# A hybrid encoder trunk on one core: seven block products in place of eight in seven GEMM stretches, and layer 1 in another order

## The chip, the core and the metric

One core of one Trainium2 chip. PE multiplies into PSUM (8 banks), ACT, DVE and POOL work on the elements, SP, ACT and POOL issue DMAs. The metric is the device time of one execution in microseconds; the kernel before took 1682.24 us (median of 3 runs, 1680.69 to 1684.24).

## The reference, cut to what matters

512 tokens, width 2048, two layers in float32. Layer 0 is latent attention with a gate, layer 1 an mLSTM with gates, each followed by an output projection and `x <- LN(ALPHA * x + y)`.

```
# layer 0: 16 heads; attn [512, 2048], z [512, 2048]
y = (attn * silu(z)) @ w_out                      # 2048 x 2048
x = layernorm(ALPHA * x + y) * ln_w + ln_b
# layer 1: 8 heads of 128 (q, k) and 256 (v)
qk, v, o, gates, z = split(x @ w_in)              # columns: 2048, 2048, 2048, 16, 2048
q, k = split(silu(causal_conv(qk)))
cell = rmsnorm(mlstm_chunkwise(q, k, v, gates))   # per head, decay exponents from the gates
y = (sigmoid(o) * cell * silu(z)) @ w_out
x = layernorm(ALPHA * x + y) * ln_w + ln_b
```

## The kernel before, in words

Every GEMM keeps float32 accuracy with three products: each operand is split into `hi` (rounded to the float32r mantissa) and `lo` (the rest), and `mm3` (L199) issues hi x hi, hi x lo, lo x hi, each a matmul of 128x128 by up to 128x512. `split` (L166) is a cast on ACT (L168) and a subtraction on DVE (L169). The activations stand transposed in SBUF, 16 k tiles of [128, 512 tokens] as `hi`/`lo` pairs (32 tiles of tag `h`). Weights come by SP's queue in units of 512 KB into three `raw` buffers (`weights`, L172) and are split into three `whi`/`wlo` pairs.

There are two loops over units. `gemm_a` (L221) has tokens as rows of the result and 512 columns; a unit of two k tiles serves every token block asked for, 24 matmuls for four blocks, 12 for two. `gemm_b` (L205) has 256 columns as rows of the result and all 512 tokens beside them. Four PSUM banks (`acc`) hold GEMM results, four (`ps`) the rest.

Work of other engines and small matmuls is written as tasks (generators) that `tick` (L116) steps between the parts of a GEMM: a task yields how many us of matmul time its next step should lie ahead. `finish` (L125) runs a task out at once. The framework then puts the instructions of each engine into an order by its own model of the times, so program order is a priority, not the order on the engine; on the chip each engine runs its list in order.

`out_proj` (L585) does four column blocks of 512: blocks 0 and 1 for all tokens, 2 and 3 for tokens 0-255 and then for 256-511, so that the first pair can be normalised (`finish0` L857, `finish1` L928) while the second is multiplied. Its input tiles are made on demand, two ahead (`g0` L881, `g1` L902).

`mlstm` (L798) goes by pairs of heads: values (`v_block`, 512 columns), o and z of the first head (`gate_out`, L694), q, k with the convolution (`conv_silu`, L682), then o and z of the second head. The cells of the two heads (`cell`, L725) are tasks beside the next GEMMs, one at a time. A cell makes four score blocks, four value steps (`values`, L745) and turns the normalised rows (`turn`, L766), multiplying by the gate. Finished heads 0 to 5 go to DRAM and come back in `g1`. The residual of layer 1 is reread from DRAM, scaled and shifted on POOL in `resid1` (L918).

Of the kernel before, what the change touches and what calls it, by code (L numbers as in the profile page):

```python
# [16 lines left out]
P = 128  # L17
# [29 lines left out]
def _pieces(value, bits):  # L47
    """The value as a sum of len(bits) + 1 float32 numbers, the first of so many bits each."""
    out = []
    for b in bits:  # L50
        e = math.floor(math.log2(value)) - b + 1
        p = math.floor(value / 2.0 ** e) * 2.0 ** e
        out.append(p)
        value -= p
    return out + [value]


class Task:
    """Work that is traced between the steps of a GEMM: a generator that yields how many us of TensorE
    time its next step should lie ahead, so that the other engines' work hides behind the GEMM."""  # L60
# [5 lines left out]
class Ahead:  # L66
    """A list whose items are made, in order, some items before they are first asked for."""
# [13 lines left out]
class Kern:  # L81
    def __init__(self, ctx, tc):
# [11 lines left out]
        self.queue, self.active = [], []  # L94

# [5 lines left out]
    def start(self, gen):  # L101
        """A task that takes its first step at once and no place among the others."""
# [57 lines left out]
    def behind(self, ins, after):  # L160
        """Instructions are issued behind earlier ones of their engines."""
# [4 lines left out]
    def split(self, src, hi, lo):  # L166
        """src = hi + lo exactly, hi being src rounded to the float32r mantissa."""
# [4 lines left out]
    def weights(self, src):  # L172
        """src: DRAM [128, kts, ..] of at most 1024 values a partition."""
# [25 lines left out]
    def mm3(self, out, a, b, start, stop):  # L199
        """out += a.T @ b, a and b pairs (hi, lo)."""  # L200
# [4 lines left out]
    def gemm_b(self, w, row0, col0, x, ncol=2, kts=4):  # L205
        """[128 * ncol columns, 512 tokens] as ncol PSUM tiles; x: list of (hi, lo) [128, 512]."""
# [44 lines left out]
    def rsqrt_small(self, a, w=1):  # L251
        """a ** -0.5 of a [128, w] tile."""
# [5 lines left out]
    def newton(self, y, a, t, eng):  # L258
        """One step for y = a ** -0.5; t is scratch."""
# [6 lines left out]
    # ---------------------------------------------------------------- constants  # L266
# [46 lines left out]
    def rope_tables(self, positions):  # L313
        """cos [128, 512] and sign * sin, row p of frequency p % 32."""
# [30 lines left out]
    def rope(self, src, n, use):  # L345
        """Rotates src (PSUM or SBUF, [n, 512], heads of 64 rows) and hands a float32 tile to use."""
# [55 lines left out]
    def mla(self, x, positions, w_in, w_qb, w_kvb, load_params):  # L402
# [34 lines left out]
        # k_rope: hi and lo of the weights side by side as the stationary operand  # L437
# [27 lines left out]
        # the gate path  # L465
# [10 lines left out]
        # attention, four heads at a time  # L476
        qv = w_qb.rearrange("(k p) (h c) -> p k h c", p=P, c=QK)
        kv = w_kvb.rearrange("(k p) (h c) -> p k h c", p=P, c=2 * NOPE)
        for grp in range(H0 // 4):
            hs = slice(4 * grp, 4 * grp + 4)  # L480

            # V in [tokens, 4 heads * 128]
# [17 lines left out]
            for pair in range(2):  # L500
# [34 lines left out]
                for j in range(2):  # L535
# [3 lines left out]
                    g[i] = g[i], self.add(self.attend(qt[j], kt[j], qr[j], (krh, krl), vs, g[i], rot))  # L539
        return g  # L540

    def attend(self, q, k, qr, kr, vs, g, rot):
        """g *= softmax(q k) v, transposed."""
# [37 lines left out]
        nc.vector.tensor_tensor(g, o, g, op=ALU.mult)  # L581

    # ---------------------------------------------------------------- output projection and LayerNorm

    def out_proj(self, w_out, g, resid, finish, last=1):  # L585
# [4 lines left out]
        nc = self.nc  # L590
        r, tasks = {}, []
# [206 lines left out]
    def mlstm(self, w_in, x, gscr, late):  # L798
        """The cells as tasks; late is x for who reads the second pair of token blocks first."""
        tasks = []  # L800
        for pair in range(H1 // 2):
# [11 lines left out]
            if pair == 0:  # L813
                self.finish(rows)
# [158 lines left out]
```

## Time and profile before

| | |
|---|---|
| runs | 1680.69, 1682.24, 1684.24 us |
| profiled execution, first to last instruction (span) | 1679.8 us |
| median of the runs less that span | 2.4 us |
| PE busy / DVE / ACT / POOL | 98 / 54 / 37 / 12% |
| granted TensorE clock, mean | 0.997 |
| DMA moved | 202.77 MB, mean 121 GB/s |

Busy is the time in which an engine had an instruction running; matmuls overlap, so the rate of PE is read from the spacing of their starts. The profiled execution is known by its span. An instruction's line can be that of a helper (L168, L169, L196), so the tile names tell which use it is.

### The profile page before, as it was taken

How to read it: one execution, taken by the hardware profiler on the slowest of the kernel's cores; microseconds unless marked ns; L12 is line 12 of the kernel's file. 1: busy time of each engine (PE TensorE's matmuls, PEld its weight loads, DVE VectorE, ACT ScalarE, POOL GpSimd, SP SyncE). 2: the span in 40 equal slices, each digit the busy share in tenths (PEclk: the TensorE clock that was granted, in tenths of full speed). 3: DMA queues.
4: the chain of work that ended last, by engine and by line, in shares of the span. 5: the costliest groups of instructions: out<-in, count | busy, mean ns of one | idle time of the engine just before them, and what ended most of it. 6: DMA issues, size and time to landing. Idle time of an engine off the chain costs nothing. (4 is left out here: it accounts for less than half of the span.)

```text
span 1679.8 us, 20372 instructions
## 1 busy us (share of the span) xinstructions
PE 1652.9 (98%) x7706; PEld 1374.3 (82%) x7706; DVE 913.6 (54%) x1750; ACT 621.1 (37%) x952; POOL 205.1 (12%) x262
## 2 busy tenths in 40 slices
PE   8999999999999999999999999999999999999996
PEld 7888888888888888788888888888888888888874
DVE  3374222677778535876564524643365524674476
ACT  3343222454556313454334322432243322542232
POOL 1000000000000000110222101220021101336200
PEclk9999999999999999999999999999999999999998
DMA  7333333322223435674435543434535543366364
GB/s 210 105 97 101 92 97 94 101 63 57 72 74 95 138 100 181 199 233 125 123 104 107 102 97 93 109 105 108 99 110 107 98 101 92 125 201 225 130 203 156
DMA packets 173538, 202.77 MB, mean 121 GB/s; under 512 B 21928, under 2 KB 120328, under 8 KB 173440
## 3 DMA queue, kind: packets, MB, share of 16 engines
q1 hardware_dynamic: 161840, 176.84, 39.1%
q0 software_dynamic: 4688, 12.05, 2.5%
q10 hardware_dynamic: 6912, 12.59, 2.4%
q8 instruction: 60, 0.98, 0.2%
q14 instruction: 38, 0.31, 0.1%
HBM read 187.63 MB, written 11.58 MB: 119 GB/s over the span
## 5 line engine op out<-in xcount | busy, mean ns | idle before, releaser
L196 PE MATMUL acc<-h,whi 128*128 128x512 f32 x2496 | 772.9, 391 | 0.0
L169 DVE TENSOR_TENSOR wlo<-raw,whi 128x1024 fp32r<-128x1024 f32 (+1 forms) x311 | 378.6, 1218 | 508.3 <-ACT whi L168 498.0
L168 ACT CAST whi<-raw 128x1024 fp32r<-128x1024 f32 (+1 forms) x311 | 322.8, 1039 | 644.9 <-PE acc L196 563.5
L196 PEld LDWEIGHTS acc<-h,whi 128*128 128x128 f32 x2496 | 465.4, 188 | 94.7 <-issue 1.0
L196 PE MATMUL acc<-whi,h 128*128 128x512 f32 x1520 | 488.6, 393 | 0.0
L196 PE MATMUL acc<-h,wlo 128*128 128x512 f32 x1248 | 486.4, 390 | 0.0
L196 PEld LDWEIGHTS acc<-whi,h 128*128 128x128 f32 x1520 | 285.3, 188 | 58.1 <-ACT whi L168 0.9
L196 PE MATMUL acc<-wlo,h 128*128 128x512 f32 x760 | 297.2, 391 | 4.8 <-DVE wlo L169 4.8
L196 PEld LDWEIGHTS acc<-h,wlo 128*128 128x128 f32 x1248 | 234.5, 188 | 49.7
L196 PEld LDWEIGHTS acc<-wlo,h 128*128 128x128 f32 x760 | 142.9, 188 | 34.2 <-DVE wlo L169 6.9
L255 POOL TENSOR_TENSOR s<-s,mhalf 128x1 f32<-128x1 f32 x40 | 25.9, 647 | 404.9 <-DVE s L607 153.0
L351 POOL DMA_DIRECT2D e<-e x34 | 17.0, 506 | 411.1 <-DVE e L349 310.7
L196 PE MATMUL ps<-h,h 128*128 128x128 f32 (+3 forms) x288 | 60.7, 319 | 0.0
L562 ACT ACTIVATE t<-ps,s 128x128 f32<-128x128 f32 (+3 forms) x64 | 33.7, 527 | 65.2 <-DVE s L561 65.1
L193 PE MATMUL ps<-ident,t 128*128 128x128 f32 x288 | 47.5, 281 | 6.2 <-DMA t<-in_x_dram 6.0
L196 PEld LDWEIGHTS ps<-h,h 128*128 128x128 f32 x288 | 48.5, 189 | 6.3
L709 POOL TENSOR_TENSOR h<-h,e 128x512 f32<-128x512 f32 x16 | 20.6, 1290 | 261.0 <-DVE e L708 261.0
L193 PEld LDWEIGHTS ps<-ident,t 128*128 128x128 f32 x288 | 37.4, 145 | 17.7 <-issue 3.7
L689 POOL TENSOR_TENSOR e<-e,e 128x512 f32<-128x512 f32 x16 | 29.0, 1815 | 164.6 <-ACT e L688 164.6
L196 PE MATMUL acc<-whi,v 128*128 128x512 f32 x128 | 44.0, 402 | 0.0
L196 PE MATMUL acc<-v,whi 128*128 128x512 f32 x128 | 41.8, 406 | 0.0
L168 ACT CAST h<-e 128x256 fp32r<-128x256 f32 (+1 forms) x48 | 22.8, 478 | 47.3 <-POOL e L689 29.5
(184 smaller groups left out, 1342.2 us busy)
## 6 DMA issues: line engine op xcount, KB each, us to landing
raw<-in_ml_w_in_dram SPq DMA_DIRECT2D x136, 512.0 KB, 5.0
raw<-in_mla_w_out_dram SPq DMA_DIRECT2D x48, 512.0 KB, 4.0
raw<-in_ml_w_out_dram SPq DMA_DIRECT2D x48, 512.0 KB, 4.0
raw<-in_mla_w_in_dram SPq DMA_DIRECT2D x47, 512.0 KB, 3.8
t<-in_x_dram SPq DMA_DIRECT2D x16, 256.0 KB, 6.5
raw<-in_mla_w_kvb_dram SPq DMA_DIRECT2D x16, 256.0 KB, 3.2
raw<-in_mla_w_kvb_dram SPq DMA_DIRECT2D x32, 128.0 KB, 2.4
raw<-in_mla_w_qb_dram SPq DMA_DIRECT2D x32, 128.0 KB, 2.3
```

Of the source, the lines that this page charges most:

```text
L168: a = self.nc.scalar.copy(hi, src)
L169: b = self.nc.vector.tensor_tensor(lo, src, hi.bitcast(F32), op=ALU.subtract)
L193: self.nc.tensor.transpose(out, in_, ident)
L196: self.nc.tensor.matmul(out, lhsT, rhs, start=start, stop=stop)
L255: nc.gpsimd.tensor_tensor(y, a, self.mhalf[:, :w], op=ALU.pow)
L351: nc.gpsimd.dma_start(s[r ^ 32 : (r ^ 32) + 32], b[r : r + 32])
L562: nc.scalar.activation(pt[bi], s[:, :n], AF.Exp, bias=b, scale=scale, accum_out=tot)
L689: nc.gpsimd.tensor_tensor(a, a, y, op=ALU.mult)
L709: nc.gpsimd.tensor_tensor(y, y, t, op=ALU.mult)
```

## The change

`quad` multiplies 512 tokens by two column blocks c0 and c1 of 512. The tokens (two halves), the k tiles (even and odd) and the columns (c0, c1) make 2 x 2 blocks, and Winograd's form of Strassen's scheme takes seven block products, p1 to p7, of sums of blocks. `combos` makes the sums of the activations on POOL, once per layer and GEMM input (`S`); the sums of the weights are made on POOL and DVE as the units arrive. The call has three parts of eight units: p1, p3; then p5, p7, p6; then p2, p4. Weight blocks are read again in each part that needs them. The two groups of four PSUM banks change roles from call to call (`banks`).

Seven calls use it: column blocks 1 and 2 of both output projections, values 512 to 1535, and for each of four pairs of heads o (512 columns) with z (512 columns). The rest of the projections stays in `gemm_a` (block 0 whole, block 3 for each half of the tokens).

Layer 1 goes in another order: all values, then all gates, both spilled to DRAM (`vscr` as hi and lo, `ascr` as sigmoid(o) * silu(z) in rows of tokens), then q, k and cells for the four pairs. A cell loads its gate rows and multiplies by them ahead of the turn. The scaled residual is made by a task beside q and k and spilled (`x1r`). Docstrings are removed.

```diff
+    def combos(self, te, to, alloc):
+        G = self.nc.gpsimd
+        a11, a21, a12, a22 = te[:, 0:256], te[:, 256:512], to[:, 0:256], to[:, 256:512]
+        G.tensor_tensor(a11, a21, a11, op=ALU.subtract)
+        G.tensor_tensor(a21, a21, a22, op=ALU.add)
+        G.tensor_tensor(a22, a22, a11, op=ALU.add)
+        G.tensor_tensor(a12, a12, a22, op=ALU.subtract)
+        ...    # te and to are split into hi, lo from alloc()
+    def quad(self, w, c0, c1, x, S, third, done):
+        first, second = self.banks
+        self.banks = second, first
+        def mul(ps, a, i, hl, j):
+            for b in range(2):
+                s = slice(b * P, (b + 1) * P)
+                self.mm3(ps[b], (a[0][:, s], a[1][:, s]), (half(hl[0])[j], half(hl[1])[j]), i == 0, i == KT // 2 - 1)
+            self.tick()
+        p1, p3 = two(first), two(first)
+        for i in range(n):
+            t = raw(blk(2 * i, c0), blk(2 * i + 1, c1))
+            hl = pair()
+            self.split(t, *hl)
+            mul(p1, toks(x[2 * i], 0), i, hl, 0)
+            mul(p3, toks(S[i][1], 0), i, hl, 1)
+        e1 = two(self.t)
+        ...    # e1 <- p1 by ACT
+        e3 = [third(b, p3[b]) for b in range(2)]
+        p5, p7 = two(second), two(second)
+        for i in range(n):
+            t = raw(blk(2 * i, c0), blk(2 * i + 1, c1))
+            b12 = self.e()
+            nc.sync.dma_start(b12, blk(2 * i, c1))
+            b11, b22 = half(t)
+            t2.append(self.t())
+            G.tensor_tensor(b22, b12, b22, op=ALU.subtract)
+            G.tensor_tensor(t2[i], b11, b22, op=ALU.subtract)
+            V.tensor_tensor(b11, b12, b11, op=ALU.subtract)
+            hl = pair()
+            self.split(t, *hl)
+            mul(p5, toks(S[i][0], 1), i, hl, 0)
+            mul(p7, toks(S[i][0], 0), i, hl, 1)
+            if i % 2:
+                ...    # t2[i-1], t2[i] are split side by side; p6 = two(first)
+                    mul(p6, toks(S[i - 1 + j][1], 1), i - 1 + j, hl, j)
+        u2, u5 = two(self.t), two(self.t)
+        for b in range(2):
+            V.tensor_tensor(u2[b], p6[b], e1[b], op=ALU.add)
+        for b in range(2):
+            V.tensor_tensor(u5[b], p5[b], u2[b], op=ALU.add)
+            G.tensor_tensor(e3[b], e3[b], u5[b], op=ALU.add)
+            V.tensor_tensor(u2[b], p7[b], u2[b], op=ALU.add)
+        for b in range(2):
+            done(b, 1, e3[b], None)
+            done(2 + b, 1, u5[b], p7[b])
+        p2, p4 = two(first), two(first)
+        for i in range(n):
+            t = raw(blk(2 * i + 1, c0))
+            b21, t4 = half(t)
+            G.tensor_tensor(t4, b21, t2[i], op=ALU.subtract)
+            ...    # split; p2 and p4 with x[2i+1], tokens 0 and 1
+        for b in range(2):
+            done(b, 0, e1[b], p2[b])
+            done(2 + b, 0, u2[b], p4[b])
     def out_proj(self, w_out, g, S, resid, finish, last=1):
+        plain((0, 1, 2, 3), 0)             # then r[tb, 0] to DRAM
+        def done(tb, col, t, ps):
+            if ps is not None:
+                e = self.e()
+                resid(tb, 1 + col, e)
+                V.scalar_tensor_tensor(e, e, ALPHA, ps, op0=ALU.mult, op1=ALU.add)
+                G.tensor_tensor(t, t, e, op=ALU.add)
+            V.bn_stats(stats[tb][:, 1 + col], t)
+        self.quad(w_out, 512, 1024, g, S, third, done)
+        for toks in ((0, 1), (2, 3)):
+            ...    # r[tb, 0] back from DRAM
+            plain(toks, 3, last if toks[0] else 1)
+            ...    # moments, task finish(toks)
     def mlstm(self, w_in, x, gscr, late, background):
+        self.values_out(w_in, x, 0, (0, 1), vscr)
+        self.values_out(w_in, late, 0, (2, 3), vscr)
+        late.close()
+        combos = self.add(self.mlstm_combos(x, S))   # a step: hi + lo of two tiles on POOL, combos
+        rows = self.start(self.gates(w_in, x))
+        self.values_out(w_in, x, 1536, (0, 1, 2, 3), vscr)
+        self.finish(combos)
+        self.quad(w_in, O_V + 512, O_V + 1024, x, S, copied, value)
+        self.finish(rows)
+        for pair in range(H1 // 2):
+            def gate(tb, col, t, ps):
+                if ps is not None:
+                    nc.vector.tensor_tensor(t, t, ps, op=ALU.add)
+                e = self.e()
+                nc.scalar.activation(e, t, AF.Sigmoid)
+                if col:
+                    nc.gpsimd.tensor_tensor(t, t, e, op=ALU.mult)
+                    z[tb] = t
+                else:
+                    nc.gpsimd.tensor_tensor(t, e, z[tb], op=ALU.mult)
+                    nc.sync.dma_start(at(ascr, tb, pair * 512), t)
+            self.quad(w_in, O_O + pair * 512, O_Z + pair * 512, x, S, copied, gate)
+        self.start(background)             # the residual: 16 tiles, 8 us apart
+        for pair in range(H1 // 2):
+            vs = self.v_block(vscr, pair)  # loads
             q_ps = self.gemm_b(w_in, 0, pair * 256, x)
             ...    # q, k, convolution as before
+                cell = self.cell(hd, q[j], k[j], vs, ascr, out, gscr if pair < 3 else None)
     def cell(...):
+        d = self.decays(hd)
+        ...    # gate rows from ascr on SP
+        yield 5.0
-            V.tensor_scalar(t, hp[:, 0:DV], y, None, ALU.mult)
+            V.scalar_tensor_tensor(t, hp[:, 0:DV], y, gate(tb), op0=ALU.mult, op1=ALU.mult)
-                V.scalar_tensor_tensor(gate[j][:, ts], tp[:, j * P : (j + 1) * P], ...)
+                nc.scalar.activation(out[j][:, ts], tp[:, j * P : (j + 1) * P], AF.Copy, scale=self.head_norm(2 * hd + j))
```

## Rows read from the trace of the kernel before

**Rows 1.** The page, busy time of each engine: us, share of the span, instructions.

```profile
PE 1652.9 (98%) x7706; PEld 1374.3 (82%) x7706; DVE 913.6 (54%) x1750; ACT 621.1 (37%) x952; POOL 205.1 (12%) x262
```

**Rows 2.** Timeline of PE inside a GEMM: start us, us, engine, line, operation, count.

```profile
966.03 0.61 PE L196 MATMUL acc<-h,whi 128*128 128x512 f32 x2
...
966.71 0.61 PE L196 MATMUL acc<-h,whi 128*128 128x512 f32 x2
```

**Rows 3.** Chain of waits, last projection, in order of time: start us, us, what.

```profile
1520.76 95.23 PE acc L196 x420
...
1658.52 1.42 PE acc L196 x5
```

**Rows 4.** Stretches: span, length; busy PE, PEld, DVE, ACT, POOL; clock, DMA share, GB/s.

```profile
586.00:629.00 43.00, 43.00 (x192) 35.59 (x191) 14.24 (x16) 8.27 (x8) 0.00 (x0) 1.00 0.32 101
651.00:673.00 22.00, 22.00 (x99) 18.22 (x98) 12.33 (x14) 8.58 (x9) 0.00 (x0) 1.00 0.61 193
677.00:700.00 23.00, 23.00 (x112) 18.54 (x111) 19.43 (x41) 9.12 (x15) 6.20 (x9) 1.00 0.77 252
1620.00:1680.00 60.00, 43.86 (x187) 34.30 (x185) 46.33 (x82) 13.85 (x15) 3.99 (x4) 0.92 0.51 174
```

**Rows 5.** Timeline of ACT in a half block; in brackets the idle time before.

```profile
653.82 1.05 ACT L168 CAST whi<-raw 128x1024 fp32r<-128x1024 f32 x1 [1.66 <-PE acc L196]
```

**Rows 6.** Timelines of POOL and of DVE where both have two-operand work.

```profile
1468.30 3.44 POOL L924 TENSOR_TENSOR t<-t,h 128x512 f32<-128x512 f32 x2
...
1469.81 0.79 DVE L169 TENSOR_TENSOR h<-g_raw,h 128x512 fp32r<-128x512 f32 x1 [0.39 <-ACT h L168]
...
1528.30 3.54 POOL L924 TENSOR_TENSOR t<-t,h 128x512 f32<-128x512 f32 x2
...
1537.79 3.52 POOL L923 TENSOR_TENSOR t<-t,h 128x512 f32<-128x512 f32 x2
1541.28 2.54 POOL L924 TENSOR_TENSOR t<-t,h 128x512 f32<-128x512 f32 x2
...
1529.95 1.27 DVE L601 SCALAR_TENSOR_TENSOR t<-t,acc 128x512 f32<-128x512 f32 x2
...
1538.55 1.62 DVE L169 TENSOR_TENSOR wlo<-raw,whi 128x1024 fp32r<-128x1024 f32 x1 [3.77 <-ACT whi L168]
```

**Rows 7.** The page, DMA issues: queue, count, KB each, median us to landing.

```profile
raw<-in_ml_w_in_dram SPq DMA_DIRECT2D x136, 512.0 KB, 5.0
...
raw<-in_ml_w_out_dram SPq DMA_DIRECT2D x48, 512.0 KB, 4.0
```

**Rows 8.** Groups by line and form: shapes, count, busy us, mean ns, idle before.

```profile
L169 DVE TENSOR_TENSOR wlo<-raw,whi 128x1024 fp32r<-128x1024 f32 x301 | 371.7, 1236 | 508.3 <-ACT whi L168 498.0 <-DMA raw<-in_mla_w_qb_dram 4.2 <-PE ps L196 4.2
...
L169 DVE TENSOR_TENSOR h<-acc,h 128x512 fp32r<-128x512 f32 x48 | 32.5, 685 | 10.6 <-ACT h L168 10.0
...
L601 DVE SCALAR_TENSOR_TENSOR t<-t,acc 128x512 f32<-128x512 f32 x32 | 21.0, 681 | 10.2 <-PE acc L196 10.1
...
L169 DVE TENSOR_TENSOR h<-e,h 128x256 fp32r<-128x256 f32 x32 | 13.2, 419 | 1.4 <-ACT h L168 1.4
...
L685 DVE TENSOR_SCALAR e<-acc,par 128x512 f32<-128x512 f32 x16 | 12.9, 806 | 5.1 <-PE acc L196 5.1
...
L876 DVE TENSOR_SCALAR e<-ps,par 128x256 f32<-128x256 f32 x24 | 12.7, 538 | 0.0
...
L935 DVE SCALAR_TENSOR_TENSOR t<-t,s,h 128x512 f32<-128x512 f32 x16 | 11.8, 742 | 0.0
...
L861 DVE TENSOR_SCALAR t<-t,s,s 128x512 f32<-128x512 f32 x16 | 8.2, 568 | 0.0
```

**Rows 9.** Timeline of DVE, one value step of the last head.

```profile
1505.62 0.15 DVE L755 COPY s<-ps 128x1 f32<-128x1 f32 x1
...
1509.19 0.48 DVE L764 TENSOR_SCALAR e<-ps,s 128x256 f32<-128x256 f32 x1
```

More of the change, by code (lines that the diff above doesn't have):

```diff
@@ L264, in newton @@
         return y
+    def combos(self, te, to, alloc):
[5 more added lines that the diff above has]
+        G.tensor_tensor(a12, a12, a22, op=ALU.subtract)
+        out = []
+        for t in (te, to):
+            hi, lo = alloc(), alloc()
+            self.split(t, hi, lo)
+            out.append((hi, lo))
+        return out
@@ L580, in attend, with out_proj, plain @@
             self.mm3(o[:, kb * P :], vs[kb], (hi[kb], lo[kb]), kb == 0, kb == NTB - 1)
[L581 to L585 removed]
+        z = g[0]
+        if not there:
+            g[0] = self.e()
+        nc.vector.tensor_tensor(g[0], o, z, op=ALU.mult)
+    def out_proj(self, w_out, g, S, resid, finish, last=1):
         nc = self.nc
+        V, G = nc.vector, nc.gpsimd
         r, tasks = {}, []
         stats = {tb: self.const.tile([P, 4, 6], F32, tag="bn", bufs=4, name=self.name("bn")) for tb in range(NTB)}
[L593 to L594 removed]
+        scr = self.dram.tile([SEQ, 512], F32, name=self.name("rscr"))
+        rows = lambda tb: scr[tb * P : (tb + 1) * P, :]
+        def plain(toks, cb, last=1):
             for tb in toks:
@@ L723, in decays, with cell @@
         return d
-    def cell(self, hd, d, q, k, vs, gate, gscr):
+    def cell(self, hd, q, k, vs, ascr, out, gscr):
         nc, V = self.nc, self.nc.vector
+        d = self.decays(hd)
+        a2 = [self.t().rearrange("p (b c) -> p b c", c=DV) for _ in range(2)]
+        for i in range(2):
+            src = ascr[2 * i * P : (2 * i + 2) * P, hd * DV : (hd + 1) * DV]
+            nc.sync.dma_start(a2[i], src.rearrange("(b p) c -> p b c", p=P))
+        gate = lambda tb: a2[tb // 2][:, tb % 2]
+        yield 5.0
         part = self.part
@@ L800, in mlstm @@
         tasks = []
+        self.start(background)
         for pair in range(H1 // 2):
-            if pair == 0:
-                vs = self.v_block(w_in, x, 0, (0, 1))
-                vs.update(self.v_block(w_in, late, 0, (2, 3)))
-                rows = self.add(self.gates(w_in, x))
-            else:
-                vs = self.v_block(w_in, x, pair, (0, 1, 2, 3))
-            gate = self.gate_out(w_in, x, 2 * pair)
+            vs = self.v_block(vscr, pair)
             q_ps = self.gemm_b(w_in, 0, pair * 256, x)
@@ L812, in mlstm @@
             k = [self.conv_silu(k_ps[j], 8 + 2 * pair + j) for j in range(2)]
-            if pair == 0:
-                self.finish(rows)
             for j in range(2):
                 hd = 2 * pair + j
-                if j:
-                    gate = self.gate_out(w_in, x, hd)
-                cell = self.cell(hd, self.decays(hd), q[j], k[j], vs, gate, gscr if pair < 3 else None)
+                out = [self.h() if hd < H1 - 1 else self.e() for _ in range(2)]
+                cell = self.cell(hd, q[j], k[j], vs, ascr, out, gscr if pair < 3 else None)
                 t = self.add(cell, 0.0 if j else 4.0)
-                tasks.append((t, gate))
+                tasks.append((t, out))
         return tasks
@@ L882, in f, with salloc @@
         def f():
-            t, task = g[i]
-            K.finish(task)
+            K.finish(g[i][1])
+            t = g[i][0]
             hi, lo = K.h(F32R), K.h(F32R)
             K.split(t, hi, lo)
+            if i % 2:
+                S0.append(K.combos(g[i - 1][0], t, salloc(i // 2)))
             return hi, lo
         return f
-    first, second = K.out_proj(mla_w_out[0], Ahead([g0(i) for i in range(H0)], 2), resid0, finish0)
+    def salloc(i):
+        return (lambda: K.v(F32R)[:, :SEQ]) if i in (0, 1, 7) else (lambda: K.h(F32R))
+    S0 = []
+    first, second = K.out_proj(mla_w_out[0], Ahead([g0(i) for i in range(H0)], 2), S0, resid0, finish0)
     K.finish(first)
     K.width = 1
-    cells = K.mlstm(ml_w_in[0], x1, gscr, Turned())
     def bcast(src, cb):
```

188 lines of the change are left out of this document (129 added, 59 removed).

## The prediction

> **What bounds the kernel now.** I read the busy shares first: PE is busy for 98% of the span, POOL for 12% [rows 1]. A busy PE need not be PE at its rate, so next the timeline of PE inside one GEMM: the triple of one `mm3` (its two matmuls on `whi` merged in one row; the one on `wlo` stands between the two rows shown) comes back every 0.68 us, 966.03 to 966.71 [rows 2], so a 128x512 matmul costs 0.227 us. Then the stretches between: through 95.23 us of the last projection, whole and half column blocks alike, the chain of waits is one row of 420 matmuls and nothing else [rows 3], 0.227 us each again, here with the weights as the moving side; it ends at the last matmuls at 1658.5, some 21 us ahead of the end of the span. So the program is PE from end to end, apart from a tail, and a matmul less is 0.227 us less, as long as the other engines keep feeding it. The reader is to see in the windows what feeding means [rows 4]: in a whole block of four token blocks (586 to 629) one weight unit of 512 KB serves 24 matmuls, DVE is busy 14 of 43 us and DMA moves 101 GB/s; in a half block (651 to 673) the same unit serves 12, DVE 12 of 22 us, DMA 193 GB/s, and PE still shows no gap. In that half block ACT waits 1.66 us of each 2.72 (12 matmuls) for PE to give back a weight buffer [rows 5]: the supply is ahead and throttled by PE.
>
> **What it removes.** One `quad` takes two column blocks of 512. Before, that was 8 block products of 48 matmuls (8 k pairs x 2 token blocks x 3), after it is 7. Each call saves 48 x 0.227 = 16 triples x 0.68 = 10.9 us, and there are 7 calls (two projections, one for values, four for gates): **-76.2 us**. The remaining matmuls have the same shape, only the side on which weights stand changes for the gates, and both forms run at 0.227 us [rows 2, 3]. 76.2 us of PE time, 336 matmuls, stay in each call.
>
> **What it adds: the supply of the calls.** First part of a call (p1, p3): 8 units of 512 KB, a split each, 12 matmuls = 2.72 us each. That is the half block of [rows 4] and [rows 5] again; I cost it at nothing, and what hides it is that same PE time.
> Second part (p5, p7, p6): 8 units of 18 matmuls = 4.08 us. Each needs two subtractions on POOL and one on DVE (128x512), the split of 1024 columns, and half of a split of two 512s. No row shows such a mixture, but its pieces are there: POOL's 128x512 two-input operations follow each other at 2.54/2 = 1.25 us when left alone; with a 1024-wide DVE split beside them two of them take 3.52 us, 0.98 more; with two 512-wide splits 3.44 (of which one row is shown, stretched to 0.79), so 0.45 for each; the DVE operations that read PSUM add nothing (3.54 us, although two L601 ran there too, is again one 1024 split) [rows 6]. And DVE's own split stretches from 1.22 to 1.62 beside POOL. So DVE with two SBUF operands and POOL take turns. Their turns add up, per unit: 2 x 1.25 + 0.98 + 2 x 0.45 = 4.38 us against PE's 4.08, so 0.30 x 8 = 2.4 us too much per call.
> Third part (p2, p4): 8 units of 2.72 us, one POOL subtraction and one split: 8 x (1.25 + 0.98) = 17.8 us of turns against 21.8. But the recombination stands there as well: two POOL additions and, in the gate calls, four POOL products (7.5 us); in the projections 2 + 2 additions (5.0 us); for the values two additions and four 512-wide DVE differences (2.5 + 1.8). Sums 25.3, 22.8 and 22.1, over by 3.5, 1.0 and 0.3 us.
> Over the call: gates 5.9, projections 3.4, values 2.7; times 4, 2 and 1 that is 33 us. From it goes the lead with which the second part starts. With three raw and three split buffers the first unit of it can be split some 1.6 us early (its load starts when unit 5 of the first part is split, about 2.3 us into PE's unit 3; landing 4.5, POOL 2.5, DVE 0.7, ACT 1.05 make 11.0 + waits of about 1 = 12.0, PE asks at 13.6): 7 x 1.6 = 11. I take **+22 us**. Below: 0, if recombination products slip behind the operands of later units and the lead is two units. Above: the ring of three raw buffers. A buffer is held for landing (4.0 us for w_out, 5.0 for ml_w_in [rows 7]), 0.4 of issue, POOL 2.6, DVE 0.7, ACT 1.05, DVE 1.22, 10.9 to 12.4 us with short waits, a third of which is 4.1, under the 4.38 above; with a full foreign turn at every step 14, a third 4.67, and in the third part 9.5, a third 3.17 against 2.72: (0.29 + 0.45) x 8 x 7 = 41 more, so 74 at the top.
> The Trainium skill has a rule on this port: "SBUF — State Buffer", section "Who interferes with whom", says that a DVE instruction with two SBUF inputs contends with a GpSimd instruction that reads SBUF, and that the pair is held for the whole instruction. By whole durations a unit of the second part would cost 5.16 us instead of 4.38. The rows agree with the taking of turns and differ in the size, 0.98 added by an operation of 1.24.
>
> **PSUM banks.** p2 finds banks free, p4 takes those of p6. After p6's last matmul DVE needs two additions (0.68 each, as L601 [rows 8]) while PE has p2's six matmuls, 1.36 us: 0.2 us late, 1.4 if a split is just under way. 0.7 x 7 = **+5** (1 to 10). At the other joints the four banks in use were emptied a part earlier.
>
> **Between the layers.** The two half blocks at the end of the projection become one per token pair, so the second pair's normalising comes 22 us after the first's instead of 44. From the first moments to the end of the late values block PE has 3 half blocks = 65 us and 4 us of transposes. DVE has 24 splits of 1.24 = 29.7, the turning of x: 16 x (0.54 + 0.42) = 15.4 and, with half on ACT, 8 x 0.54 + 16 x 0.42 = 11, 16 normalisations of 0.57 = 9.1, and 8 evacuations of 0.7 = 5.6: 71 us [rows 8]. Level with PE; before it was 19.4 of 23 at the worst [rows 4]. **+4** (0 to 8). The sums S for layer 1 (POOL, 8 x (2 x 1.25 + 4 of half the width) = some 42 us plus turns) lie beside 43.5 us of values and 19 us of p1/p3; nothing, at most 8 if that cover is short.
>
> **The cells.** Four pairs of q and k (43.5 us of GEMM) now follow each other with no gate GEMM between. DVE per pair: 8 splits 9.9, four convolutions of four passes of at most 0.81 and a split of 0.69, 3.9 [rows 8], so 15.6, and two cells, each four value steps of 2.2 [rows 9] and some 4 us for scores and their splits (eight operations of 0.3 to 0.7), 12.8: 51 us in 43.5 + 13 of PE. It just fits, **+5** (0 to 15) for cells that arrive late. The residual's POOL work (16 x 2.5 us) moves here from the last projection; POOL, busy for 12% before [rows 1], has room, and behind it stand the cells' decay loads and square roots, each due 5 us ahead or four to a cell. The values and gates come back through SP's queue, 8 and 2 loads of 256 KB a pair and head; what waits on SP behind them are weights with three buffers.
> The last head: the cell starts about 27 us into the last projection's first block instead of at its start, because head 6 is no longer covered by head 7's gates. The block asks for it after six units, 33 us and the cells' own 5. By then the scores are traced; the four value steps (4.07 us from L755 to the end of L764, DVE occupied 2.2 of them [rows 9]: 4.1 + 3 x 2.2), the turn and the split, 13 us, lie beside one unit of 5.4. **+7** (2 to 12).
>
> **The tail.** LayerNorm of the first token pair (8 x 2 x 0.74 = 11.9 us of DVE [rows 8]) had 43.5 us of PE beside it and now has 21.8, where 8 splits take 9.9: 21.8 of 21.8, and the last block waits on splits. **+4** (0 to 10). The 21 us after the last matmul stay.
>
> **Sum**, against the profiled execution's span: 1679.8 - 76.2 + 22 + 5 + 4 + 5 + 7 + 4 = 1650.6. The three runs' median, 1682.24, is 2.4 above that span, so 1653.
>
> **Rivals.**
> (a) The lead hides the supply: parts two and three cost nothing, the other terms at their lower half (12 us): 1682.2 - 76 + 12 = 1618. For it: half blocks of the same DMA rate ran without a gap [rows 3, 4]. Against it: POOL does nothing in those.
> (b) Slower: POOL and DVE block each other for whole instructions. Place: parts two and three of each call. 2.54 for POOL's two, 1.24 and 2 x 0.69 for DVE's [rows 6, 8] make 5.16 a unit, 41.3 us, and 8 x (1.27 + 1.24) + 7.5 = 27.6 for gates (25.1 projections, 25.4 values) against 54.4 of PE: 14.5, 12.0 and 12.3 over, 94 in all; with the other 25 us 1682 - 76 + 119 = 1725. It decides from (76.2 - 25)/7 = 7.3 us a call on; the ring of three raw buffers with full foreign turns, 74 instead of 22, ends on the same side at 1705. For it: 4.38 already exceeds 4.08. Against: 0.98 and 0.45 as measured. (The Trainium skill's page named above states it so.)
> (c) The dense ends (cells, transition, tail) at their upper bounds, 8 + 15 + 12 + 10 = 45 instead of 20: 1678, the gain all but eaten.
> (d) The calls don't save PE time, since small gaps let the granted clock fall from 2.4 to 1.2 GHz as it partly does in the last 60 us (0.92 there [rows 4]): every us at the low level costs half a us. A few gaps of 7 us would have to recur in each call; 1690.
>
> **How the numbers follow.** Forecast 0.50 (its own range 1634 to 1671), (a) 0.22, (b) 0.12, (c) 0.12, (d) 0.04. About 0.2% (3.4 us) is what a measurement of this kernel tells from no change. Faster: all of the forecast and (a), and most of (c): 0.82; same: a sixth of (c) and the edges of (b), 0.04; slower 0.14. The range 1619 to 1690 leaves out the lower part of (a) and the most of (b).
>
> **What would show it.** Right: about 336 matmuls fewer; PE gaps of 0.5 to 5 us at the start of each third part and within the second, behind DVE `wlo` and POOL; POOL two-input operations of 1.3 to 2.3 us filling the second parts; a gap of some 7 us before the last units of the last projection's first block. Wrong: PE unbroken through the calls (a), a second part of over 41 us (b), PE waiting for cells pair after pair (c), a granted clock under 0.97 in the calls (d). The prediction fails if the calls lose under 1 or over 7 us each.

## The result: 1.166 times the time of before

| | us |
|---|---|
| before, median of 4 runs | 1681.82 (1680.69 to 1684.24) |
| after, median of 4 runs | 1960.68 (1957.36 to 1968.47) |
| ratio | 1.1658, interval 1.1633 to 1.1684 |
| predicted | 1653 (1619 to 1690) |

The profiled execution spans 1966.8 us at a mean granted clock of 0.931. The page after, busy shares, slices of the span and chain:

```profile
PE 1688.8 (86%) x7370; PEld 1361.3 (69%) x7370; DVE 1194.8 (61%) x1942; ACT 747.2 (38%) x1187; POOL 625.5 (32%) x600
...
PE   8999999999998898966988788886897788758885
...
PEclk9999999999998998987999989997898899878898
...
PE 42%; DVE 17%; DMA 15%; POOL 13%; issue 7%; ACT 4%; SPq 1%; POOLq 0%; DVEq 0%; ACTq 0%
```

The 336 matmuls are gone (7706 before [rows 1], 7370 now), but from the 13th slice on PE is no longer busy from end to end, and only 42% of the ending chain is PE. From the start times of the matmuls the span can be taken apart: full-rate time (0.227 us for 512 columns), what pauses add, and what intervals near double length add (the spacing of the lower clock level). Before: about 1613 + 14 + 35 us; after: about 1540 + 301 + 105. So some 287 us more went into pauses and 70 into matmuls at the lower clock level.

Windows of the changed kernel (span, length; busy PE, PEld, DVE, ACT, POOL; clock, DMA share, GB/s): second part of the first projection's quad, first part of the values' quad with a long wait in it, second part of the second gate quad, then q, k and cells up to the last q, k matmul, and the first block of the last projection behind it:

```profile
623.00:675.00 52.00, 42.78 (x154) 32.55 (x153) 31.40 (x28) 15.81 (x20) 24.09 (x17) 0.84 0.41 127
...
870.00:923.00 53.00, 25.30 (x86) 18.47 (x85) 26.87 (x24) 17.80 (x27) 35.65 (x33) 0.71 0.47 129
1119.00:1178.00 59.00, 40.37 (x155) 31.41 (x154) 30.94 (x27) 17.20 (x23) 27.59 (x19) 0.83 0.61 111
1420.00:1662.00 242.00, 210.20 (x966) 174.22 (x965) 146.45 (x314) 99.24 (x172) 97.27 (x113) 0.94 0.61 155
1662.00:1800.00 138.00, 89.95 (x400) 71.04 (x399) 90.31 (x264) 61.37 (x139) 49.93 (x76) 0.83 0.38 116
```

The whole column block of [rows 4] had PE busy for 43 of 43 us at clock 1.00. Here no engine is full and the DMAs are not either: a chain of waits, not a rate, in every one. The seven second parts, each from the end of the first part's last matmul to the end of its own last and so with the wait ahead of it, take 50.0, 43.0, 45.1, 56.8, 46.0, 56.6 and 48.3 us, 345.7 together, where I had 8 x 4.08 = 32.6 each and 2.4 more. (The expectations below had a few matmuls of the neighbouring parts in the count, 52 us a part.)

In that of the third gate quad (1227 to 1274) the longest waits are these (us in all, times, longest):

```profile
DVE raw L340 <- POOL t L339: 14.2, 4, 8.5
ACT whi L169 <- DVE raw L340: 13.6, 5, 5.4
POOL raw L338 <- DMA raw<-in_ml_w_in_dram: 11.5, 2, 6.9
```

They make a ring: POOL waits for the load, DVE for POOL, the cast for DVE, and the next load for a buffer that the cast and the split give back. SP's timeline there:

```profile
1221.49 2.06 SPq L304 DMA_DIRECT2D raw<-in_ml_w_in_dram  x4
1233.02 2.61 SPq L335 DMA_DIRECT2D e<-in_ml_w_in_dram  x3
1236.48 1.93 SPq L304 DMA_DIRECT2D raw<-in_ml_w_in_dram  x4
```

And POOL's:

```profile
1227.46 2.54 POOL L338 TENSOR_TENSOR raw<-e,raw 128x512 f32<-128x512 f32 x2 [2.31 <-issue]
1229.96 4.16 POOL L339 TENSOR_TENSOR t<-raw 128x512 f32<-128x512 f32 x3
1241.01 1.30 POOL L338 TENSOR_TENSOR raw<-e,raw 128x512 f32<-128x512 f32 x1 [6.89 <-DMA raw<-in_ml_w_in_dram]
```

SP issues nothing from 1223.6 to 1233.0. In its list the `e` loads of the next three units stand ahead of the first of their `raw` loads, and `e` has three slots, given back by DVE's subtraction. So the units go in batches of three, with a dead time for loading after each.

What a pause does to PE, ahead of the second part of the fourth gate quad, PE's timeline:

```profile
1327.62 0.39 PE L197 MATMUL ps<-whi,h 128*128 128x512 f32 x1
...
1341.27 1.22 PE L197 MATMUL acc<-whi,v 128*128 128x512 f32 x2 [13.25 <-ACT whi L169]
...
1344.19 0.63 PE L197 MATMUL acc<-whi,v 128*128 128x512 f32 x1
...
1344.62 0.63 PE L197 MATMUL acc<-wlo,v 128*128 128x512 f32 x1
...
1345.05 0.55 PE L197 MATMUL acc<-whi,v 128*128 128x512 f32 x1
...
1345.67 0.39 PE L197 MATMUL acc<-whi,v 128*128 128x512 f32 x1
```

After 13 us without work the matmuls come every 0.43 us (1.2 GHz), and every 0.23 us (2.4 GHz) from about 1345.4 on.

### The profile page after: what moved, and what is told of

It is laid out like the page before. It is cut to its first block, busy times and chain, and to the rows that moved or that the text cites. A ratio compares the mean times of both kernels' runs of the same rounds, so it can differ in the third digit from the quotient of the medians.

```text
span 1966.8 us, 21494 instructions
## 1 busy us (share of the span) xinstructions
PE 1688.8 (86%) x7370; PEld 1361.3 (69%) x7370; DVE 1194.8 (61%) x1942; ACT 747.2 (38%) x1187; POOL 625.5 (32%) x600
## 4 chain that ended last, share of the span: by engine, by line
PE 42%; DVE 17%; DMA 15%; POOL 13%; issue 7%; ACT 4%; SPq 1%; POOLq 0%; DVEq 0%; ACTq 0%
PE acc L197 33%; DMA raw<-in_ml_w_in_dram 8%; PE ps L197 8%; DVE wlo L170 7%; ACT whi L169 3%; DMA raw<-in_ml_w_out_dram 2%; PE ps L194 2%; DMA h<-n 1%; DMA raw<-in_mla_w_out_dram 1%; DVE raw L340 1%; POOL raw L367 1%; DVE h L170 1%; POOL e L951 1%; POOL t L339 1%; POOL s L256 1%
## 5 line engine op out<-in xcount | busy, mean ns | idle before, releaser
L170 DVE TENSOR_TENSOR wlo<-raw,whi 128x1024 fp32r<-128x1024 f32 (+1 forms) x351 | 476.0, 1362 | 373.9 <-ACT whi L169 360.6
L197 PE MATMUL acc<-h,whi 128*128 128x512 f32 x1472 | 461.9, 395 | 0.0
L197 PEld LDWEIGHTS acc<-h,whi 128*128 128x128 f32 x1472 | 276.6, 190 | 56.0 <-issue 1.0
L197 PE MATMUL acc<-h,wlo 128*128 128x512 f32 x736 | 288.9, 393 | 0.0
L197 PE MATMUL ps<-whi,h 128*128 128x512 f32 x568 | 192.7, 410 | 20.7 <-ACT whi L169 12.5
L197 PEld LDWEIGHTS acc<-h,wlo 128*128 128x128 f32 x736 | 139.4, 189 | 29.6
L197 PEld LDWEIGHTS ps<-whi,h 128*128 128x128 f32 x568 | 112.7, 199 | 48.3 <-ACT whi L169 16.3
L197 PE MATMUL ps<-wlo,h 128*128 128x512 f32 x284 | 119.2, 420 | 26.9 <-DVE wlo L170 26.9
L367 POOL TENSOR_TENSOR raw<-raw,t 128x512 f32<-128x512 f32 x56 | 82.6, 1486 | 74.8 <-DMA raw<-in_ml_w_in_dram 41.7
L197 PE MATMUL ps<-whi,v 128*128 128x512 f32 x168 | 65.5, 451 | 42.3 <-DVE ones L822 22.7
L197 PEld LDWEIGHTS acc<-whi,v 128*128 128x128 f32 x296 | 59.4, 203 | 47.1 <-ACT whi L169 32.9
L339 POOL TENSOR_TENSOR t<-raw 128x512 f32<-128x512 f32 x56 | 84.6, 1520 | 2.8
```

The source lines that it names most:

```text
L170: b = self.nc.vector.tensor_tensor(lo, src, hi.bitcast(F32), op=ALU.subtract)
L197: self.nc.tensor.matmul(out, lhsT, rhs, start=start, stop=stop)
L339: G.tensor_tensor(t2[i], b11, b22, op=ALU.subtract)
L367: G.tensor_tensor(t4, b21, t2[i], op=ALU.subtract)
```

## The experiments

GpSimd is POOL, VectorE is DVE, the array is PE. The theories: A, the latency of the weight sums' chain through three buffers, with SP's order as its worst part; B, GpSimd and VectorE taking turns at their shared port (B1: the turns alone; B2: VectorE's full queue); C, the loads themselves; D, a low clock that a quad leaves behind; E, too little dense work beside the cells; F, the residual's work on POOL.

**e1_order**: the order on SP and POOL.

```
 b12 = self.e()
-nc.sync.dma_start(b12, ...)
+after(nc.sync.dma_start(b12, ...), "sp")    # raw loads too; after(): behind the one before
-G.tensor_tensor(b22, b12, b22, ...)         # and the second subtraction
+after(G.tensor_tensor(b22, b12, b22, ...), "pool")
```

> Change kept whole; only the order on two queues is forced in the second part of each quad: on SP a unit's b12 load stands right behind its three raw loads and the units go in sequence; on GpSimd a unit's two subtractions stand one behind the other. Theory A (the second part is bound by latency, because SP stops at a load that waits for one of e's slots and the raw loads behind it start late): the second part falls from a mean of 52 us to 33 to 40, seven times 12 to 19, and the kernel comes to 1830 to 1880 us. Theory B (port turns between GpSimd and VectorE make the unit longer whatever the order): the second part stays at 45 or more, 1915 to 1965 us. Theory C (the transfers from the packed weights are the limit): it stays at 50, 1950 us or more.

Measured 1937.4, ratio 1.152 [1.146, 1.158]. Second parts 325.6 together (42.3 to 55.1 each): 20 less than 345.7. The order on SP and POOL cost only that, 23 us of the whole; A in its form "order" fails.

**e2_nosums**: no sums of weights.

```
-G.tensor_tensor(b22, b12, b22, ...); G.tensor_tensor(t2[i], b11, b22, ...)
-V.tensor_tensor(b11, b12, b11, ...)
-t2.append(self.t())
+t2.append(b12)          # third part: split b21 twice
```

> Left out of the computation: the sums and differences of weight blocks (the split takes the blocks as they are loaded); the seven products, the loads and their bytes stay. Theory A (supply chain with GpSimd's subtractions in it): the second part falls to 33 to 36 us and the third to 22, some 7 x 20 = 140 us, 1800 to 1840 us. Theory B (port turns): the same fall, since GpSimd has nothing left to do there. Theory C (the same bytes have to come in): the second part stays at 45 us or more and the kernel over 1920 us.

Measured 1839.7, ratio 1.094 [1.088, 1.100]. Second parts 247.3, five of the seven at 32.9 or 33.0 without a pause. C falls: the same bytes arrive in time. The weight sums cost 121 us (1960.7 less 1839.7): by the matmuls' times 98 of it in the second parts and 24 in the third (196.2 to 171.8). But with the sums gone the kernel is still 158 us slower than before, so most of the loss is elsewhere.

**e3_proj**: quads in the two projections alone.

```
 # kernel before + combos, quad, out_proj, g0, g1 of the changed kernel; mlstm as before
-    def out_proj(...):                # 8 products
+    def out_proj(..., S, ...): ...; self.quad(w_out, 512, 1024, g, S, third, done); ...
```

> Only the two output projections go by seven products; layer 1 stays in its old order, without spills, sums of its activations or quads. Theory A/B (quads cost 25 to 30 us more each than eight products' time, the rest of the loss comes from layer 1): the projections lose 2 x 16 to 2 x 25 us against the kernel before, 1705 to 1735 us. Theory D (the cost is the stretch behind the quad, where the clock stays low): over 1740 us. If the quads in the projections are worth what they leave out: below 1675 us.

Measured 1776.9, ratio 1.057 [1.053, 1.060]: worse than A and B said, and in the range of D. But low clock is not the bulk of it: pauses are 87 us more than before, time at the low level 28. Two quads cost 95 us net, and by the loads' times 24 us of it have fallen by the last load of the first projection, 16 more by the last load of layer 1's input weights, and 53 between that load and the last matmul.

**e4_plain8**: eight products in the changed order.

```
 def quad(...):
-    ...
+    for col, c in ((1, c1), (0, c0)):
+        out = self.gemm_a(w, c, x, (0, 1, 2, 3))
+        for tb in range(NTB): done(tb, col, third(tb, out[tb]), None)
```

> Eight products in every place where the changed kernel has seven (two plain column blocks a call), no sums of activations; layer 1 in the changed order, with the spills. Theory E (taking the gate GEMMs out from between the cells leaves nothing dense beside the cells' chains, and the cells' stretch is the second large loss): 1755 to 1800 us, with the q, k and cells stretch still near 325 us. Theory A alone (everything comes from the quads' supply, cells lose because of what the quads leave behind): 1682 to 1720 us.

Measured 1795.6, ratio 1.068 [1.065, 1.071]: the order of layer 1 alone costs 114 us, in E's range; A alone is out. The projections are plain here, and the gate GEMMs run without a pause (800 to 1300: PE busy 500 of 500 us, clock 1.00). Then q, k and cells to the last q, k matmul, and the first block of the last projection:

```profile
1300.00:1518.00 218.00, 184.99 (x850) 153.72 (x849) 130.25 (x298) 90.14 (x161) 87.77 (x108) 0.91 0.57 152
1518.00:1645.00 127.00, 89.60 (x411) 72.14 (x410) 75.03 (x251) 52.75 (x123) 21.98 (x44) 0.84 0.51 158
```

Pauses and low clock add 47 us in the first window and 56 in the second. At the last q, k matmul the value steps of four of the eight heads are still to come (before: of one), and the block that follows takes its operands from these cells.

**e5_dummy**, **e13_pooldummy**, **e14_dvedummy**: e2_nosums plus subtractions that nobody reads.

```
 self.split(t, *hl)
+f = half(hl[0])[0].bitcast(F32)
+G.tensor_tensor(d[0], d[0], f, ...)    # twice; e14: V;   third part: once
+V.tensor_tensor(d[1], d[1], f, ...)    # not in e13
```

> The kernel without sums of weight blocks, plus subtractions of the same number and size whose results nobody reads: GpSimd two and VectorE one per unit of the second part, GpSimd one per unit of the third, each after the unit's cast, on tiles of their own (left out of the computation: the sums themselves). The engines and their port are as loaded as in the changed kernel; no load and no product waits for a subtraction. Theory B (the shared port and the load of the engines make the unit long): the second part goes back from 35 us to 43 or more and the kernel from 1840 to 1890 or more. Theory A (the latency of load, two subtractions, third subtraction, cast, split through three raw buffers): the second part stays at 34 to 38 us, the kernel at 1840 to 1860 us.

> The kernel without sums of weight blocks, plus GpSimd's subtractions that nobody reads (two per unit of the second part, one per unit of the third), without VectorE's; left out of the computation: the sums themselves. VectorE has only its splits to do, 1.24 + 0.68 us a unit, so only the turns at the shared port can make it late. Theory B1 (the port's turns alone): nearly as slow as with VectorE's subtractions too, part two at 41 to 45 us, 1890 to 1930 us. Theory B2 (VectorE's queue is full, and the turns only add to it): part two stays at 35 to 39 us, 1840 to 1870 us.

> The same with all the unread subtractions on VectorE and none on GpSimd: three a unit of the second part beside the splits, 4.0 us a unit against 4.08 us of the array, one a unit of the third; left out of the computation: the sums themselves. No turns at the port. Theory B1 (turns): part two 35 to 38 us, 1840 to 1865 us. Theory B2 (VectorE's own load, each split queued behind subtractions that are not urgent): 40 to 45 us, 1880 to 1910 us, as with the real sums on VectorE (44 us, 1911).

Measured 1929.9 (ratio 1.147 [1.144, 1.150]), 1903.0 (1.132 [1.129, 1.135]) and 1853.4 (1.103 [1.096, 1.109]). The second part of the same gate quad in windows (window, length, then PE, PEld, DVE, ACT, POOL busy, clock, DMA share, GB/s), e2:

```profile
1160.20:1194.30 34.10, 34.10 (x151) 27.98 (x150) 16.82 (x20) 15.01 (x22) 0.00 (x0) 1.00 0.48 143
```

e5:

```profile
1204.60:1243.90 39.30, 35.88 (x150) 27.42 (x149) 38.95 (x27) 14.95 (x23) 31.64 (x18) 1.00 0.40 117
```

e13:

```profile
1191.40:1225.40 34.00, 34.00 (x150) 27.95 (x149) 30.56 (x20) 14.87 (x22) 31.06 (x18) 1.00 0.45 135
```

e14:

```profile
1161.40:1195.50 34.10, 34.10 (x151) 28.00 (x150) 31.99 (x48) 15.62 (x23) 0.00 (x0) 1.00 0.51 150
```

the changed kernel:

```profile
1227.10:1274.20 47.10, 37.48 (x150) 29.24 (x149) 32.34 (x27) 16.59 (x21) 27.36 (x18) 0.93 0.37 109
```

DVE's splits alone are 17 us; POOL beside them stretches the same splits to 31; DVE's own subtractions make it 32; both together fill DVE, 38.95 of 39.30 us. Neither B1 nor B2 as stated: in the second part (252.9 and 255.6 us in all, against 247.3, and 289.4 with both) it takes DVE's queue and the turns together. DVE's timeline of e5:

```profile
1215.71 1.77 DVE L346 TENSOR_TENSOR t<-t,whi 128x512 f32<-128x512 f32 x1
1217.41 2.31 DVE L170 TENSOR_TENSOR wlo<-raw,whi 128x1024 fp32r<-128x1024 f32 x1
...
1228.66 1.22 DVE L170 TENSOR_TENSOR wlo<-raw,whi 128x1024 fp32r<-128x1024 f32 x1
1229.79 0.68 DVE L346 TENSOR_TENSOR t<-t,whi 128x512 f32<-128x512 f32 x1
```

POOL's:

```profile
1217.01 1.62 POOL L344 TENSOR_TENSOR t<-t,whi 128x512 f32<-128x512 f32 x1
1218.71 2.15 POOL L345 TENSOR_TENSOR t<-t,whi 128x512 f32<-128x512 f32 x1
```

Beside POOL every DVE operation takes 1.09 us more, whatever its own length (0.68 to 1.77, 1.22 to 2.31); alone (1228.7 to 1230.4, POOL idle) nothing. It is nearly a whole POOL operation of 1.25 us each time; one operation of each comes round in 1.70 or 2.23 us, 0.23 less than the two alone would take one behind the other. Of the 63 us by which e13 is over e2, 43 lie in the third parts (28 to 37 us each against 23 to 28) and 6 in the second; its unread subtractions read a split buffer and may hold it there, so that share is not the port's for certain.

**e6_dve**: all weight sums on VectorE, loads in order.

```
-G.tensor_tensor(b22, b12, b22, ...); G.tensor_tensor(t2[i], b11, b22, ...)
+V.tensor_tensor(b22, b12, b22, ...); V.tensor_tensor(t2[i], b11, b22, ...)   # t4 too
```

> The changed kernel with all four sums of weight blocks on VectorE in place of GpSimd, the loads in the order of their units. VectorE then has about 0.68 x 3 + 1.24 + 0.68 = 4.0 us a unit of the second part against 4.08 us of the array. Theory A (latency): the chain is shorter by two subtractions at 0.7 in place of 1.5 us, so the second part falls to 37 to 42 us; the kernel to 1865 to 1905. Theory B (port): the second part falls to 34 to 36 us, the kernel to 1840 to 1860. A third reading (VectorE's rate takes over): the second part stays at 45 us or more, 1930 us or more.

Measured 1910.8, ratio 1.136 [1.132, 1.139]; second parts 295.4. With the port out of it and DVE busy as in e14, the real sums take 295 where the unread ones take 256: the difference is the data they wait for.

**e7_raw4**: a fourth raw buffer.

```
-N_T = 16, N_RAW = 3
+N_T = 14, N_RAW = 4
```

> The changed kernel with four raw weight buffers in place of three and 14 t tiles in place of 16 (the room for it). Theory A (three buffers held some 11 us each, from the load's issue to the split, allow a unit each 4 to 6 us): the second part falls by a quarter, 52 to about 40 us, and the kernel by 50 to 80 us, to 1880 to 1910. Theory B (rate of the shared port): within 15 us of 1961. If the t tiles become the limit, the joint between second and third part gets longer and the time rises.

Measured 1924.9, ratio 1.144 [1.139, 1.149]: 36 us less, where A said 50 to 80. Second parts 335.4, only 10 less; 16 came from the first parts of the gate quads, 22 to 23 us where they had 25 to 28. So the number of `raw` buffers alone does not set the second part as it stands; a fourth slot for `e` was not tried.

**e8_resid**: e4_plain8 with the residual's multiply and add back in `resid1`.

```
-self.start(background)          # residual(): 16 x (load, 2 POOL operations, store)
+resid1: n1 loaded, G.tensor_tensor(t, t, w, mult), G.tensor_tensor(t, t, b, add)
```

> The kernel with eight products everywhere and layer 1 in the changed order, with one more edit: the residual's multiply and add stand again at the reader in the last projection, not as a background task of GpSimd beside the cells. Theory F (the in-order queue of GpSimd, held by the residual's loads, makes the cells' chains late): the stretch of q, k and cells falls from about 320 to 270 us or less, the kernel to 1735 to 1755. Theory E (too little dense work beside the cells, whoever shares GpSimd): under 15 us less, 1780 to 1796.

Measured 1776.3, ratio 1.056 [1.053, 1.059]: 19 us, between F and E. POOL's queue was a part of the cells' loss, not the main one; 93 us of the order remain. Pauses and low clock are down to 16 us beside q and k (47 in e4) and at 65 in the last projection's first block behind them (56): what is left of the cells' loss is mostly their lateness at the end.

**e9_nogates**: the kernel before without gate GEMMs.

```
 def gate_out(...):
-    o_ps = self.gemm_b(...) ; z_ps = self.gemm_b(...) ; ...
+    for _ in range(2): y = self.h(); V.memset(y, 1.0); out.append(y)
```

> The kernel before with the gates' GEMMs left out (ones in the place of the gate tiles): in the old order, but with the cells standing beside the q, k and value GEMMs alone. Left out are 8 heads x 192 matmuls x 0.227 us = 348 us of the array. Theory E (without the gates' products the cells' chains have nothing dense to stand beside): the array idles where it did not before, and the time falls by 230 to 300 us only, to 1380 to 1450 us. If the changed order loses by its spills and reloads or by its rows of loads instead: it falls by 335 to 350, to 1332 to 1347 us.

Measured 1374.9: 306 us less, where 348 us of matmuls went. In its intervals full-rate time falls by 348, pauses rise by 32 and low-clock time by 12. In the old order too the cells lose 42 us once the gates' products don't stand beside them: E, just under the range I gave. Most of it, 30 us, stands behind the last q, k matmul (1137 to 1240), with two heads' value steps still to come; beside q, k and values (800 to 1137) it is 15. In the changed order the values are missing there as well, and spills and reloads are added; what either adds was not measured by itself.

**e10_ssums**: layer 1's activation sums on VectorE.

```
 def mlstm_combos(...):
-    G = self.nc.gpsimd
+    G = self.nc.vector
```

> The changed kernel with the sums of layer 1's activations on VectorE in place of GpSimd (48 operations of 512 and 256 columns); all else as it is. Theory: the 23 us in which the array stands still ahead of the first quad of layer 1 are the chain of these sums on GpSimd, some 50 us long, that starts when the normalised rows are there; on VectorE, beside the casts and splits of the plain value block, it is half as long: the stillstand falls to under 8 us, the kernel to 1930 to 1945 us. Rival (the stillstand is the copies and splits of the sums, or the gates' rows, which stay): within 8 us of 1961.

Measured 1940.7, ratio 1.154 [1.149, 1.158]; as the theory said. The first part of the values' quad falls from 57.6 to 32.8 us.

**e11_first**: the kernel before with one quad, in the first projection, with e6's supply.

```
-first, second = K.out_proj(mla_w_out[0], ...)
+first, second = K.out_quad(mla_w_out[0], ..., S0, resid0, finish0)   # sums on V, loads in order
```

> The kernel before with seven products in the first output projection alone, there with the cheapest form of the supply found so far (sums of weights on VectorE, loads in their order). By the quad's own stretch (41.6 + 18.4 + 29.8 against 87.2 us for eight products) nothing is gained or lost inside it; what is left is the first column block beside the sums of activations (+13 us of gaps) and the joint behind: 1690 to 1710 us. If the quad pays once its supply is right: under 1680 us. If layer 1 is hit by what the quad leaves behind (late tiles, slots): over 1715 us.

Measured 1707.5, ratio 1.015 [1.011, 1.019]: in the range. Even this single quad loses 27 us, with 10.9 us of matmuls saved.

**e12_all** and **e15_all4**: all remedies (e6's sums and order of loads, e10, e8); then four raw buffers too.

```
-G.tensor_tensor(...)            # weight sums, layer 1's activation sums
+V.tensor_tensor(...)
-self.start(background)          # the residual back in resid1
-N_T = 16, N_RAW = 3             # e15 alone
+N_T = 14, N_RAW = 4
```

> The changed kernel with all the remedies together: weight sums on VectorE with the loads in their order, layer 1's activation sums on VectorE, the residual's arithmetic back at its reader. If the causes add: 1961 - 50 - 20 - 22 = 1870 us (1850 to 1890). If they share a cause (VectorE's load moves from one place to the other): over 1900 us. In no case under the kernel before, since the changed order alone with eight products and the residual moved back takes 1776 us and the quads lose on top of it.

> All remedies together (weight sums and layer 1's activation sums on VectorE, loads in order, residual back at its reader) with four raw weight buffers and 14 t tiles. Theory A (what is left in the quads is the latency through three buffers): another 20 to 35 us less than 1885, 1850 to 1865 us. Theory B2 (VectorE's load): within 10 us of 1885. In both cases over 1776 us, the time of the changed order with eight products.

Measured 1884.9 (ratio 1.121 [1.116, 1.125]) and 1843.3 (1.097 [1.093, 1.100]). The remedies nearly add: 76 us together, 89 by the single runs. With the port out of the way the fourth buffer gives 42 us, more than A's 35, and 29 of it in the second parts (302.7 to 273.5): there three buffers were a limit. What is left is not shown to be the ring alone: in e15 all parts of the seven calls together still take 117 us more than their matmuls at full rate. It is the best version with seven quads and stays 67 us above e8, which has none. No version here that computes the whole result beats the kernel before.

## Why the prediction was wrong, by its steps

From runs, if the steps add up (no run tests that for all of them), the way from before to after (+279) is about: products -76; layer 1's order +114 (e4; 19 of it the residual, e8); GpSimd's and VectorE's unread work +90 (e5 over e2); waiting for the real sums +31 (after over e5); activation sums of layer 1 +20 (e10). That leaves about +100 for the quads without weight sums. The traces show where it lies: with layer 1's activation sums e2 has 89 us more pauses than e4 and 29 more at low clock, of these 84 in the calls for values and gates (35 of them in the first part of the values' call), 20 in the first projection and behind it, 13 from the cells to the end. No run isolates their causes.

- **What it removes, -76.2**: right, 336 matmuls.
- **Supply, +22 (0 to 74)**: the step that failed first; the weight sums cost 121 (after over e2). Two parts were wrong. My turns, 0.98 for a 1024 split and 0.45 for a 512, are what POOL loses; in e5 it goes from 1.25 to 2.15 and 1.62, +0.90 and +0.37. DVE loses 1.09 at each operation in the same turn and that I did not add up on DVE's side, where it fills the engine: three operations of 1.22, 0.68 and 0.64 and two turns of 1.09 make 4.72 us a unit (my estimate from e5's rows), 37.8 a part, and e5's shortest five are 38.2 to 40.2. I had read DVE's stretch as 1.22 to 1.62; the trace of before already had a longer one beside POOL's operations:

```profile
1554.54 2.32 DVE L169 TENSOR_TENSOR wlo<-raw,whi 128x1024 fp32r<-128x1024 f32 x1 [3.66 <-ACT whi L168]
```

The price comes near that of rival (b): its 5.16 us a unit make 41.3 a part, and its 94 us in all stand against 90, though part of the 90 lies in third parts and may be held buffers (e13). The Trainium skill has the pair held for a whole instruction ("SBUF — State Buffer", section "SBUF: two separate sides"), a rule that I set aside for the smaller number. In e5 1.09 us is added beside an operation of 1.25, which nearly agrees with it. Second, I counted the ring of three raw buffers at 4.1 us a unit, each step at its own duration. In fact units wait for each other in order, on SP, POOL and DVE: 49.4 us a part, 6.2 a unit. Which of these waits, or of the slots behind them, sets it is open: forced order gave 23 us, a fourth buffer 36.
- **First part, nothing**: wrong. 25 to 28 us in the gate quads against 21.8, and 22 to 23 with a fourth buffer.
- **PSUM banks, +5 (1 to 10)**: not as a delay of every call. PE waits for these additions in one call alone, the last gate quad's, 7.9 us.
- **Between the layers, +4 and the sums S at nothing (at most 8)**: the normalising has about 15 us more of pauses and low clock in e4 (690 to 800) than before (640 to 760). S cost 20 by e10. The cover I named, 43.5 us of values and 19 of the first part, could not hold: the first part's p3 takes S from its first unit on, so PE stood for 23 us:

```profile
PEld ps L197 <- DVE ones L822: 23.2, 1, 23.2
```

The row names the gates' rows; e10, which moved only the sums, took the wait away.
- **Cells, +5 (0 to 15), and last head, +7 (2 to 12)**: an error as large as the supply's, 114 by e4 with the transition in it. I compared DVE's busy time with PE's; but the chain of a cell (value step, square root on POOL, turn) leaves DVE idle while it waits. Waits of the changed kernel, 1420 to 1745:

```profile
POOL s L256 <- DVE s L892: 38.4, 17, 4.4
...
PE ps L194 <- DVE e L895: 26.0, 8, 8.6
POOL h L1112 <- DMA h<-n: 24.9, 5, 5.9
```

PE waits for the rows to turn in its own order, with the next GEMM behind the wait; the residual's operation waits on POOL for a load, with the cells' work behind it. So the cells fall behind q and k. I had the last head, and little of the one before, left for the last projection's first block; four of the eight have their value steps behind the last q, k matmul (1662), the last at 1783, and pauses and low clock add 45 us from 1420 to 1662 and 70 from there to 1800.
- **The end of the trace of before**: I took the last matmuls to stand at 1658.5. They go on to 1666.7, 13 us ahead of the end; the sum does not use the difference.
- **Clock, rival (d) at 0.04**: it came as a companion of all the others, +70 us. I had priced it as an alternative; it is a surcharge on pauses. The 0.92 that I took for a sign of it was none: before, the clock is 1.00 from 1620 to 1670 and falls only behind the last matmul (0.55 from 1670 to 1680). The gaps of 7 us in its condition came from no row.
- **Rival (a)** was wrong, **(c)** right in kind at a third of the size (45 us where the order and the sums S cost 134), **(b)** near in size for the turns, and too narrow a place for the whole.

## What to carry to other kernels

Where the array is busy from end to end, the other engines' idle time is cover, and an edit that saves matmuls spends it: cost the new supply as a ring (buffers over the time that one is held, with in-order waits), not by busy sums. Sum turns at a shared port on both engines. Work beside a latency-bound chain has a value of its own: e9 lost 42 us by removing GEMMs. Ask how far such chains lag when the GEMM that needs their results begins: here four cells of eight were late.

## What the runs showed of the hardware

While both had work waiting (e5, 1215.7 to 1228.7), 128x512 POOL subtractions and DVE operations with two SBUF operands came one for one: DVE +1.09 us, POOL +0.37 or +0.90 by the length of DVE's. Loads were no limit: 143 GB/s in e2's second part, without a pause. In the changed kernel 287 us more of pauses came with 70 us more in matmuls near the 0.43 us spacing of the 1.2 GHz level.
